# A decoder block on one core: two entries held back at the stage boundaries, and eight turns of the identity at the start

## The chip, the cores and the metric

The kernel runs on one core of a Trainium2 chip. A core has engines with a queue of instructions each, which run beside one another and wait for each other through semaphores: TensorE (PE in the profile, its weight loads PEld), VectorE (DVE), ScalarE (ACT), GpSimd (POOL) and SyncE (SP, which here only issues DMAs). An engine takes its own instructions in order, so one that waits holds up all behind it. The metric is the device time of one execution in microseconds.

## The reference

One layer of a hybrid decoder on x of 256 tokens by 2048 channels, all in float32:

```python
x = layer_norm(ALPHA * x + 0.5 * swiglu(x, ffn1...), ln1_g, ln1_b)
mix = concat(attention(x @ w_in), rg_lru(x @ w_in)) @ w_out
x = layer_norm(ALPHA * x + mix, ln2_g, ln2_b)
x = layer_norm(ALPHA * x + 0.5 * swiglu(x, ffn2...), ln3_g, ln3_b)
x = x + sigmoid(x @ w_ple_gate) * (p @ w_ple_proj)
```

swiglu is (silu(x @ gate) * (x @ up)) @ down with a width of 5632. The layer norm is taken over the 2048 channels of a token: mean and variance, then a scale and a shift per channel. Each stage needs the normalised output of the stage before.

## The kernel before, in words

**Numbers in two halves.** TensorE multiplies in a rounded float32 format. Each operand is therefore split into hi (its rounded value, a cast on ScalarE, line 104) and lo (the rest, a subtraction on VectorE, line 109), and a product is hi*hi + hi*lo + lo*hi.

**The plan.** All weights stand in one list, self.plan, in the order in which they are used. An entry is 256 rows by 512 columns, 512 KB. load() issues its DMA into a raw tile (10 of them), prepare_hi() casts, prepare_lo() subtracts. Most entries put hi and lo into two pools of 7 slots (SLOTS); entries marked "work" put them into the pool of 11 work tiles (w4, "w" in the rows) that the stages use for their intermediate results too. Work entries are the third and fourth of the last eight of a down projection, and the first three of the next stage.

**Who prepares when.** take() hands out the next entry and calls advance(), done() gives its slot back and calls it too. advance() goes up to AHEAD = 7 entries beyond those taken, bounded by self.limit and by free slots, and issues the lo split one entry behind the hi cast:

```python
end = min(self.limit, self.taken + AHEAD)
while self.ready < end and (self.plan[self.ready]["work"] or self.live < SLOTS):
    self.prepare_hi(self.ready)
    self.ready += 1
    self.advance_lo(self.ready - 1 if self.taken else self.ready)
```

prepare_hi(q) also issues the loads of all entries below q + 5. The order of the instructions on each engine is the order in which the Python code issues them (manual_schedule); a tile from a pool waits for the last use of the tile that had its place.

**A stage boundary, down_last (line 492).** The last 512 rows of a down projection (ffn1, w_out, ffn2: three calls) are eight entries: for each of four blocks n of 512 columns, two. The first loop takes them and sums token tile 0 (128 tokens): down_mm(acts, es[n], 0, n, False) is 12 matmuls into one bank, into_acc (line 385) adds the bank to acc on VectorE, ln_stats (513) takes statistics. ln_norm (515) aggregates them, GpSimd raises to the power -0.5 (522), and VectorE normalises acc in four pieces (525). The second loop does token tile 1 with the same entries; halfway through its block 1 TensorE transposes the first four blocks of normalised tile 0 (ln_transpose, 535: four transposes into a bank, ScalarE scales and shifts, line 538, then casts and VectorE subtracts into xT, lines 64 and 65), and after blocks 1, 2 and 3 the rest. Entries are given back in the second loop, so done() prepares more there.

**After a boundary.** The next stage begins with eight entries on token tile 0 alone (group_b with boundary=True), and transposes tile 1 during the last four of them (HOOKS); after the second call of swiglu, ple_proj with four entries comes first, which needs p and not xT. split_p, which splits p into one work tile, is part of preparing its first entry.

**The start.** setup() (line 640) writes the identity with GpSimd; self.ident is used for all transposes. Then the first entries and xT are loaded, cast and split, and TensorE begins with group_a.

Of the kernel before, what the change touches and what calls it, by code (L numbers as in the profile page):

```python
# [12 lines left out]
P = 128  # L13
# [27 lines left out]
class Block:  # L41
# [449 lines left out]

    def down_last(self, acts):
        es, st = [], [self.tile(self.small, [P, 4, 6], F32, "bst") for _ in range(2)]
        for n in range(4):
            es.append([self.take(), self.take()])
            self.down_mm(acts, es[n], 0, n, False)
            self.ln_stats(st[0], 0, n)
        self.ln_norm(st[0], 0)
        for n in range(4):
            self.down_mm(acts, es[n], 1, n, False, mid=(lambda: self.ln_transpose(0, 0)) if n == 1 else None)  # L500
            self.ln_stats(st[1], 1, n)
            if n < 3:
                for e in es[n]:
                    self.done(e)
            if n > 0:
                self.ln_transpose(0, n)
        self.ln_norm(st[1], 1)
        for e in es[3]:
            self.done(e)
# [130 lines left out]
    def setup(self):  # L640
        nc, i = self.nc, self.i
        c = self.const
        self.ident = c.tile([P, P], F32, name="ident")
        make_identity(nc, self.ident)
        self.mhalf = c.tile([P, 1], F32, name="mhalf")
        nc.gpsimd.memset(self.mhalf, -0.5)
        self.par = c.tile([P, 192], F32, name="par")
        self.trig = c.tile([P, 2, 2, 16], F32, name="trig")
        self.dec = c.tile([P, 2, 12], F32, name="dec")
# [359 lines left out]
```

## Time and profile before

| | us |
|---|---|
| median of 3 timed runs | 1912.32 (1910.5 to 1912.78) |
| the profiled execution | 1905.79 |
| its span, first to last instruction | 1904.0 |
| TensorE busy (share of the span) | 1868.5 (98%) |
| VectorE busy | 1494.9 (79%) |
| ScalarE busy | 1077.8 (57%) |
| mean granted TensorE clock | 0.995 |

The profile is of one execution. "Busy" is the time in which an engine had an instruction under way; matmuls are pipelined and their ends are modelled, so consecutive ones overlap in the rows (389 ns printed, 0.23 from start to start for 512 columns). What an engine waits for is read from the views of waits and from the instructions in order of time, where idle time before an instruction and what ended it stand in brackets. The releaser named is the one that came last by the profile, which can be a neighbour of the true one.

### The profile page before, as it was taken

How to read it: one execution, taken by the hardware profiler on the slowest of the kernel's cores; microseconds unless marked ns; L12 is line 12 of the kernel's file. 1: busy time of each engine (PE TensorE's matmuls, PEld its weight loads, DVE VectorE, ACT ScalarE, POOL GpSimd, SP SyncE). 2: the span in 40 equal slices, each digit the busy share in tenths (PEclk: the TensorE clock that was granted, in tenths of full speed). 3: DMA queues.
4: the chain of work that ended last, by engine and by line, in shares of the span. 5: the costliest groups of instructions: out<-in, count | busy, mean ns of one | idle time of the engine just before them, and what ended most of it. 6: DMA issues, size and time to landing. Idle time of an engine off the chain costs nothing.

```text
span 1904.0 us, 26424 instructions
## 1 busy us (share of the span) xinstructions
PE 1868.5 (98%) x9844; PEld 1603.2 (84%) x9844; DVE 1494.9 (79%) x1910; ACT 1077.8 (57%) x1422; POOL 124.2 (7%) x108
## 2 busy tenths in 40 slices
PE   8999999999999989999999899999999999999899
PEld 7888888888888878887888788888888888888687
DVE  6698887887888876688677867878879888788674
ACT  6565555555655646555755455655556556556552
POOL 0001010100010000011100000101000101010000
PEclk9999999999999999999999999999999999999999
DMA  9678687788786857565455575887887878778381
GB/s 354 232 198 264 203 257 235 207 260 247 211 255 209 266 178 231 175 185 158 138 184 187 167 243 155 250 231 211 258 247 207 255 211 253 243 198 276 131 263 44
DMA packets 214593, 413.02 MB, mean 217 GB/s; under 512 B 13104, under 2 KB 15808, under 8 KB 214464
## 3 DMA queue, kind: packets, MB, share of 16 engines
q1 hardware_dynamic: 193856, 370.42, 58.1%
q0 software_dynamic: 20608, 40.91, 12.6%
q8 instruction: 77, 1.26, 0.3%
q14 instruction: 52, 0.43, 0.1%
HBM read 409.18 MB, written 2.10 MB: 216 GB/s over the span
## 4 chain that ended last, share of the span: by engine, by line
PE 95%; DVE 2%; ACT 1%; issue 1%; DMA 0%; SPq 0%; POOL 0%; DVEq 0%; POOLq 0%; ACTq 0%
PE mm L264 94%; DVE lo L109 1%; PE mm L535 1%; DMA raw<-in_ffn_w_gate_dram 0%; ACT hi L104 0%; DVE w L109 0%; DVE bst L513 0%; DVE acc L385 0%; PE mm L792 0%; DVE raw L82 0%; DVE w L721 0%; DVE w L65 0%; ACT w L64 0%; POOL rs L522 0%; DVE w L627 0%
## 5 line engine op out<-in xcount | busy, mean ns | idle before, releaser
L104 ACT CAST hi<-raw 128x1024 fp32r<-128x1024 f32 (+1 forms) x774 | 797.2, 1049 | 556.4 <-PE mm L264 501.2
L264 PE MATMUL mm<-xT,hi 128*128 128x512 f32 x3072 | 1057.6, 391 | 5.6 <-ACT hi L104 5.6
L109 DVE TENSOR_TENSOR lo<-raw,hi 128x1024 fp32r<-128x1024 f32 (+1 forms) x774 | 915.2, 1221 | 93.4 <-ACT hi L104 84.5
L264 PE MATMUL mm<-xT,lo 128*128 128x256 f32 x3072 | 850.5, 277 | 0.1
L264 PEld LDWEIGHTS mm<-xT,hi 128*128 128x128 f32 x3072 | 577.5, 188 | 127.2 <-ACT hi L104 5.8
L264 PEld LDWEIGHTS mm<-xT,lo 128*128 128x128 f32 x3072 | 577.7, 188 | 6.3 <-DVE lo L109 1.3
L264 PE MATMUL mm<-hi,w 128*128 128x512 f32 x1480 | 481.6, 391 | 1.8 <-DVE acc L435 1.2
L264 PEld LDWEIGHTS mm<-hi,w 128*128 128x128 f32 x1480 | 277.9, 188 | 63.7 <-ACT hi L104 1.5
L264 PE MATMUL mm<-lo,w 128*128 128x512 f32 x740 | 289.5, 391 | 0.0
L264 PE MATMUL mm<-hi,xT 128*128 128x512 f32 (+1 forms) x648 | 200.9, 385 | 0.0
L264 PEld LDWEIGHTS mm<-lo,w 128*128 128x128 f32 x740 | 139.1, 188 | 23.9
L85 POOL DMA_DIRECT2D raw<-in_ffn_w_down_dram x72 | 86.6, 1214 | 1080.7 <-DVE raw L82 547.7
L437 DVE TENSOR_TENSOR acc<-acc,mm 128x512 f32<-128x512 f32 x110 | 75.2, 684 | 98.6 <-PE mm L264 98.6
L264 PEld LDWEIGHTS mm<-hi,xT 128*128 128x128 f32 x648 | 120.3, 188 | 23.1
L264 PE MATMUL mm<-lo,xT 128*128 128x512 f32 (+1 forms) x324 | 123.6, 382 | 0.0
L378 DVE TENSOR_TENSOR w<-mm,w 128x256 f32<-128x256 f32 x192 | 80.2, 419 | 20.5 <-ACT w L377 20.0
L82 DVE TENSOR_TENSOR raw<-raw,raw 128x1024 f32<-128x1024 f32 x72 | 87.9, 1221 | 1.2
L377 ACT COPY w<-mm 128x256 f32<-128x256 f32 x192 | 69.6, 364 | 21.2 <-PE mm L264 17.2
L64 ACT CAST w<-qk 128x512 fp32r<-128x512 f32 (+1 forms) x42 | 25.5, 609 | 86.4 <-DVE qk L482 46.0
L612 ACT ACTIVATE w<-w 128x256 f32<-128x256 f32 x84 | 35.1, 418 | 66.3 <-DVE w L378 66.3
L264 PEld LDWEIGHTS mm<-lo,xT 128*128 128x128 f32 x324 | 61.0, 188 | 11.2
L613 DVE TENSOR_TENSOR w<-w,w 128x256 f32<-128x256 f32 x84 | 35.8, 426 | 41.4 <-ACT w L612 41.4
(139 smaller groups left out, 788.0 us busy)
## 6 DMA issues: line engine op xcount, KB each, us to landing
raw<-in_ffn_w_up_dram SPq DMA_DIRECT2D x176, 512.0 KB, 4.9
raw<-in_ffn_w_down_dram SPq DMA_DIRECT2D x176, 512.0 KB, 5.3
raw<-in_ffn_w_gate_dram SPq DMA_DIRECT2D x175, 512.0 KB, 6.0
raw<-in_w_in_dram SPq DMA_DIRECT2D x88, 512.0 KB, 4.6
raw<-in_ffn_w_down_dram POOLq DMA_DIRECT2D x72, 512.0 KB, 7.6
raw<-in_w_out_dram SPq DMA_DIRECT2D x32, 512.0 KB, 4.4
raw<-in_w_ple_gate_dram SPq DMA_DIRECT2D x32, 512.0 KB, 5.6
w<-in_ln_g_dram SPq DMA_DIRECT2D x12, 256.0 KB, 7.4
```

What stands on the lines that cost most here:

```text
L64: self.nc.scalar.copy(hi, src)
L82: self.nc.vector.tensor_tensor(a, a, b, op=ALU.add)
L85: self.nc.gpsimd.dma_start(a, src, accum_op=ALU.add)
L104: self.nc.scalar.copy(e["hi"][:, k, :], e["raw"][:, k, :])
L109: self.nc.vector.tensor_tensor(e["lo"][:, k, :], e["raw"][:, k, :], e["hi"][:, k, :].bitcast(F32), op=ALU.subtract)
L264: self.nc.tensor.matmul(out, lhsT=lhsT, rhs=rhs, start=start, stop=stop, skip_group_check=True)
L377: self.nc.scalar.copy(c, bank[:, 256:])
L378: self.nc.vector.tensor_tensor(dst, bank[:, :256], c, op=ALU.add)
L437: self.nc.vector.tensor_tensor(a, a, bank, op=op)
L535: nc.tensor.transpose(bank[:, q * P:(q + 1) * P], self.acc[:, t, kb * P:(kb + 1) * P], self.ident)
L612: nc.scalar.activation(s, g, AF.Sigmoid)
L613: nc.vector.tensor_tensor(g, g, s, op=ALU.mult)
```

## The change

In down_last self.limit is set to ten entries beyond those taken, eight of its own and two of the next stage, before the first loop, and lifted after ln_norm of token tile 0. In setup a PSUM bank is taken and TensorE transposes the identity into it eight times; nothing reads that bank.

```diff
     def down_last(self, acts):
         es, st = [], [self.tile(self.small, [P, 4, 6], F32, "bst") for _ in range(2)]
+        self.limit = self.taken + 10
         for n in range(4):
             es.append([self.take(), self.take()])
             self.down_mm(acts, es[n], 0, n, False)
             self.ln_stats(st[0], 0, n)
         self.ln_norm(st[0], 0)
+        self.limit = len(self.plan)
         for n in range(4):
             self.down_mm(acts, es[n], 1, n, False, mid=(lambda: self.ln_transpose(0, 0)) if n == 1 else None)
             self.ln_stats(st[1], 1, n)
@@
         make_identity(nc, self.ident)
+        bank = self.bank()
+        for _ in range(8):
+            nc.tensor.transpose(bank[:, :P], self.ident, self.ident)
         self.mhalf = c.tile([P, 1], F32, name="mhalf")
```

## Rows read from the trace of the kernel before

**Rows 1.** The chain of work that ended last: share of the span by engine.
```profile
PE 95%; DVE 2%; ACT 1%; issue 1%; DMA 0%; SPq 0%; POOL 0%; DVEq 0%; POOLq 0%; ACTq 0%
```
**Rows 2.** TensorE's waits: waiter, releaser, us in total, times, longest.
```profile
PE mm L535 <- DVE acc L525: 19.1, 3, 8.0
```
**Rows 3.** TensorE in order of time, first call: start, us, instruction [idle before <-releaser].
```profile
696.56 0.62 PE L264 MATMUL mm<-hi,w 128*128 128x512 f32 x2
...
699.51 1.52 PE L264 MATMUL mm<-w,w 128*128 128x512 f32 x6
706.62 1.11 PE L535 MATMUL mm<-ident,acc 128*128 128x128 f32 x4 [5.59 <-DVE acc L525]
...
723.67 0.60 PE L535 MATMUL mm<-ident,acc 128*128 128x128 f32 x4
```
**Rows 4.** VectorE in order of time, first call.
```profile
700.90 1.23 DVE L109 TENSOR_TENSOR w<-raw,w 128x1024 fp32r<-128x1024 f32 x1 [6.92 <-PE mm L264]
...
703.37 0.67 DVE L385 TENSOR_TENSOR acc<-acc,mm 128x512 f32<-128x512 f32 x1
...
706.01 1.92 DVE L525 TENSOR_SCALAR acc<-acc,mv,rs 128x512 f32<-128x512 f32 x4 [0.76 <-POOL rs L522]
707.84 0.68 DVE L385 TENSOR_TENSOR acc<-acc,mm 128x512 f32<-128x512 f32 x1
...
709.17 2.34 DVE L109 TENSOR_TENSOR lo<-raw,hi 128x1024 fp32r<-128x1024 f32 x2
...
719.22 0.69 DVE L65 TENSOR_TENSOR xT<-qk,xT 128x512 fp32r<-128x512 f32 x1 [0.81 <-ACT xT L64]
...
720.94 1.92 DVE L525 TENSOR_SCALAR acc<-acc,mv,rs 128x512 f32<-128x512 f32 x4 [0.67 <-POOL rs L522]
```
**Rows 5.** VectorE in order of time, third call.
```profile
1780.64 1.23 DVE L109 TENSOR_TENSOR w<-raw,w 128x1024 fp32r<-128x1024 f32 x1 [8.71 <-ACT hi L104]
```
**Rows 6.** TensorE in order of time, second and third call.
```profile
1077.26 1.11 PE L535 MATMUL mm<-ident,acc 128*128 128x128 f32 x4 [5.49 <-DVE acc L525]
...
1788.80 1.11 PE L535 MATMUL mm<-ident,acc 128*128 128x128 f32 x4 [8.03 <-DVE acc L525]
```
**Rows 7.** A stretch: us, PE busy (instructions), granted clock, DMA share, GB/s.
```profile
706.60:710.00 3.40, 3.38 (x11) 0.52 0.00 0
```
**Rows 8.** The chain in order of time, three calls: start, us, what.
```profile
707.73 2.42 PE mm L264 x6
710.15 0.44 PE mm L535 x4
...
726.09 1.40 PE mm L264 x6
...
1078.38 2.56 PE mm L264 x6
1080.94 0.85 PE mm L535 x4
...
1789.91 2.35 PE mm L264 x6
```
**Rows 9.** All engines in order of time, the start.
```profile
1.02 0.29 POOL masks.py:199 TENSOR_SCALAR_AFFINE_SELECT ident<-ident 128x128 f32<-128x128 f32 x1
...
5.17 0.77 PE L264 MATMUL mm<-xT,hi 128*128 128x512 f32 x1 [5.17 <-ACT hi L104]
...
9.19 1.04 ACT L104 CAST hi<-raw 128x1024 fp32r<-128x1024 f32 x1 [1.05 <-DMA raw<-in_ffn_w_gate_dram]
9.23 0.63 PE L264 MATMUL mm<-xT,hi 128*128 128x512 f32 x1
...
9.87 0.51 PE L264 MATMUL mm<-xT,hi 128*128 128x512 f32 x1
...
10.27 1.22 DVE L109 TENSOR_TENSOR lo<-raw,hi 128x1024 fp32r<-128x1024 f32 x1 [1.41 <-ACT hi L104]
...
11.54 0.38 PE L264 MATMUL mm<-xT,lo 128*128 128x256 f32 x1
```

## The prediction

> **What bounds the kernel now.** I read the chain of waits first: TensorE holds 95% of it [rows 1]. So only two things can move the time: a wait of TensorE, or a stretch in which it runs slowly. The list of TensorE's waits has one large entry: three waits of L535 (the transposes of a normalised token tile) for L525 (the normalisation on VectorE), 19.1 us together, the longest 8.0 [rows 2]. They are the first transposes in the three calls of down_last. I call the calls A (about 690 to 735 us), B (1062 to 1100) and C (1769 to 1825), number the ten or so plan entries from a call's start 0, 1, 2, ... (0 to 7 are its own, 8 on belong to the next stage), and write (t, n) for the twelve matmuls of token tile t and column block n.
>
> In A TensorE ends (0,3) with the matmul started at 696.56, goes on with (1,0) and the first half of (1,1), and should transpose at 699.51 + 6 x 0.23 = 700.9; it does so at 706.62, after 5.59 idle [rows 3]. The VectorE rows say why [rows 4]: the lo split of entry 10 ("w<-raw,w") sits idle 6.92 us until 700.90, waiting for TensorE, and behind it in the queue stand into_acc and bn_stats of (0,2) and (0,3), the aggregate and the normalisation (706.01). (0,2) was finished on TensorE by 694.3 (696.56 less twelve matmuls at 0.23, and its own end). The releaser's time is the end of the first half of (1,1), the last reader of entry 2, which lies in the same pool of work tiles as entry 10: the split waits for that tile. So VectorE does no normalising until TensorE has used up everything that does not need it.
>
> **Part 1, the limit.** take() prepares up to seven entries ahead, so before the change entries 8 to 11 are prepared while tile 0 is summed. With the limit at ten, entries 10 and 11 go behind ln_norm. One more thing goes with them: the lo split is issued one entry behind the hi cast, so lo 9 is only issued when entry 10 is prepared. Ahead of ln_norm VectorE therefore keeps lo 8 and loses lo 9 and lo 10. This matters in C, where it is lo 9 that blocks (8.71 idle, start 1780.64 [rows 5]); there split_p takes one more work tile.
>
> New order on VectorE in A: lo 8, into_acc and bn_stats of (0,1), (0,2), (0,3) as TensorE delivers them. (0,3) can be added at about 697.0 (last matmul 696.56 + 0.43). From that instruction to the normalisation took 706.01 - 703.37 = 2.64, so it starts at 699.6, its first quarter (1.92/4, printed 0.56 in the chain) is out at 700.2, and TensorE arrives at 700.9 [rows 3, 4]. The 5.59 goes, with 0.6 to spare. B and C run the same matmuls in the same order, so 5.49 and 8.03 go as well [rows 6]. Sum of the waits: **19.1**.
>
> The waits cost more than their idle time. After the one in A the granted clock is 0.52 from 706.60 to 710.00, the lower of the two levels (1.2 against 2.4 GHz); the engine had stood still for 5.59 us before [rows 7]. In the chain the four transposes take 1.11 instead of 0.44, and the six matmuls after them 2.42 in A, 2.56 in B, 2.35 in C instead of 1.40; B's next four transposes take 0.85 [rows 8]. That is (0.67 + 1.02) + (0.67 + 1.16 + 0.41) + (0.67 + 0.95) = **5.6**, and without an idle stretch it goes.
>
> What the moved work costs. It is not removed: after into_acc and bn_stats of (1,0), the two done() calls now issue lo 9, 10, 11, 12 where lo 11 and 12 stood. hi 10 to hi 13 keep their order on ScalarE (no other ScalarE instruction lies between), and the loads theirs on SP's queue; raw 9 and raw 10 are held longer, but the loads that reuse them are for entries 19 and 20. lo 9 and lo 10 may now wait for entry 2's tiles, free at 700.9, while VectorE reaches them at 702.8. Two more splits are 2.3 us by the pair at 709.17 [rows 4]. into_acc of (1,0) moves from 707.84 to 701.5, 6.4 earlier; all that follows on VectorE moves 6.4 - 2.3 = 4.1 earlier, and the 0.81 idle at 719.22 closes, so the second normalisation starts at 720.94 - 4.9 = 716.0 and its first quarter is out at 716.6. TensorE gains 5.6 + 1.7 = 7.3 and reaches the first transposes of tile 1 at 723.67 - 7.3 = 716.4 [rows 3, 4]. So VectorE is next late, by some 0.2 to 0.3. B has the same order of work on both engines and is charged alike: **0.7** for the two, with the restart. In C ple_proj lies between (it needs no tile of xT): nothing. Worked on with the same durations, the split of xT's first block of tile 0 ends at about 708 (needed by the next stage at 709.7), entries 14 and 15 are split by 719.1 and 720.2 (needed at 718.7 and 720.5): covered, or short by tenths. If the cover is less, each us of VectorE's lateness costs A and B one us.
>
> **Part 2, the eight turns.** They start when the identity is there (1.02 + 0.29 = 1.31 [rows 9]). Four transposes at the low clock took 1.11 [rows 3], so eight end near 3.6, before the first matmul, which waits for data until 5.17 [rows 9]; even at 0.47 each unoverlapped they end at 5.1. Cost 0. Gain: an early pair of matmuls (512 and 256 columns) takes 0.64, as 9.23 to 9.87 shows, about twice what the six of rows 8 suggest at the higher clock, and between 7.6 and 9.87 there are three and a half pairs: about 1.0 us of TensorE time. But the next entry's weights land at 9.17, ScalarE casts from 9.19, VectorE splits from 10.27 to 11.50, and TensorE's idle ends at 11.54 with exactly that split [rows 9]; a faster TensorE waits longer for it. So 0, with bounds 0 and 1.0 gained (if that load lands an us earlier in another run).
>
> The Trainium skill speaks against this part: "TensorE: Matmul & The Clock Gate", Part 4 on the PE-mode transpose, says that transposes do not count as TensorE activity for the clock. By it the first real matmuls still take 0.64 a pair and the gain is 0 in every run; if it does not hold here, up to the 1.0 above is there for the taking. No row of before has transposes alone, so the trace does not decide; the forecast is 0 either way.
>
> **Sum.** 19.1 + 5.6 - 0.7 + 0 = 24.0 us. The profiled execution took 1905.8 (1904.0 span): 1881.8 there. The timed runs have a median of 1912.3, 6.5 above it, and I see no row that says what the 6.5 is; taking 24.0 from the median gives **1888.3**. Bounds: the waits alone with no clock gain and two us of lateness in A and B, 19.1 - 4 = 15; everything, with the start's 1.0 and no lateness, 25.7.
>
> **Rivals.**
> 1. VectorE's tail is later than I make it (a hi cast of 10 or 11 that must wait for entry 2's tiles puts four casts of 1.05 ahead of tile 0's evacuation, 0.9 later at the second normalisation in each of A and B; or lost tenths elsewhere). For it: slack of a few tenths only. Two of the three calls lose 0.9 to 1.9 each: 20 to 22 us gained, 21 in the middle: 1891.3. Chance 0.17.
> 2. The limit does not free the blocked split everywhere: if lo 9 stayed ahead of the sums, C would keep its wait but for one split (1.2 gained instead of 9.6), 15.6 in all: 1896.7. Against: the one-entry lag of the lo splits is in the code and in the order of rows 4 (lo 10 after hi 11). Chance 0.06.
> 3. It gets slower: a moved split gets a work tile that is free only at the end of (1,3), 709.1 in the new time, and holds VectorE with tile 0's xT behind it. Then xT of block 0 is ready at 713.1 instead of 707.9 and TensorE waits 3.6, then about 2 more at tile 1's transposes, and 1.7 for the clock; with the release 1 us later still A loses more than its 7.3. For all three calls: 1914 to 1917. It decides from a release at 709 on. For it: the pool is at its limit in the trace (6.92 and 8.71 idle). Against: entry 2's two tiles are free at 700.9 and entry 3's at 702.7, and only lo 9, hi 10 and lo 10 need any. Chance 0.03.
> 4. No difference: the waits go, and as much comes back at tile 1's transposes. That would need six more us on VectorE there than I count: 1912. Chance 0.02.
>
> **How the numbers follow.** Forecast 0.72, rivals 0.17, 0.06, 0.03, 0.02. About 0.2% (3.8 us) is what a measurement of this kernel can tell from no change. Faster 0.95 (forecast, rivals 1 and 2), same 0.02, slower 0.03. The range: the forecast's own, 24.0 -1.7 +1.7 +- the runs' spread (1905.8 to 1912.8 shows that a median may lie 6 lower), is 1882 to 1892; reaching to rivals 1 and 2 makes it 1882 to 1897.
>
> **What would show it.** Right: no wait of L535 for L525 above 1 us; the clock at 1.00 through all three calls; VectorE's split before the sums only lo 8; four lo splits after into_acc of (1,0); the first transposes of a call directly after the sixth matmul of (1,1). For part 2: matmuls of the first entry at 0.34 or 0.64 a pair, and TensorE's steady run starting at 11.5 in both cases. Wrong: a wait of more than 1 us at tile 1's transposes or at the next stage's first matmuls, or a start earlier than 11.

## The result, and the profile after

| | before | after |
|---|---|---|
| median of 4 timed runs | 1911.41 us (1909.25 to 1912.78) | 1885.42 us (1883.78 to 1885.59) |
| the profiled execution | 1905.79 us | 1883.78 us |
| its span | 1904.0 us | 1882.0 us |

The ratio is 0.9863, 95% interval 0.9846 to 0.988: 26.0 us less in the medians, 22.9 to 29.4 by the interval (0.012 and 0.0154 of 1911.4). Between the two profiled executions it is 22.0 us. The forecast was 1888.3 us, that is 24.0 less than the 1912.3 of three runs; the time lies in the range of 1882 to 1897.

The page of the changed kernel: granted clock in 40 slices, shares of the chain that ended last.

```profile
PEclk9999999999999999999999999999999999999999
...
PE 95%; DVE 2%; ACT 1%; DMA 1%; issue 1%; SPq 0%; ACTq 0%; DVEq 0%
```

The shares of the chain say nothing about the change: TensorE holds 95% before [rows 1] and after. The list of TensorE's waits, read next, does: here are its longest entries in the changed kernel (waiter, releaser, us in total, times, longest). The transposes of L535 stand at L537 now, the normalisation of L525 at L527.

```profile
PE mm L264 <- DVE xT L65: 1.7, 1, 1.7
PE mm L264 <- ACT w L798: 1.6, 1, 1.6
```

No entry of L537 is left in it, where 19.1 us stood [rows 2]. The windows around the calls A, B and C of the changed kernel (us, TensorE busy and instructions, granted clock, DMA share, GB/s) show that the slow stretches behind the waits [rows 7] went too:

```profile
684.00:735.00 51.00, 51.00 (x241) 1.00 0.50 160
1060.00:1105.00 45.00, 45.00 (x215) 1.00 0.51 156
1765.00:1825.00 60.00, 60.00 (x282) 1.00 0.62 206
```

How it went is seen in call A. VectorE of the changed kernel, in order of time (start, us, instruction, idle before and its releaser):

```profile
691.32 1.21 DVE L109 TENSOR_TENSOR w<-raw,w 128x1024 fp32r<-128x1024 f32 x1
...
698.00 0.69 DVE L385 TENSOR_TENSOR acc<-acc,mm 128x512 f32<-128x512 f32 x1 [1.30 <-PE mm L264]
...
700.67 1.91 DVE L527 TENSOR_SCALAR acc<-acc,mv,rs 128x512 f32<-128x512 f32 x4 [0.76 <-POOL rs L524]
...
703.82 2.34 DVE L109 TENSOR_TENSOR w<-raw,w 128x1024 fp32r<-128x1024 f32 x2
706.08 2.35 DVE L109 TENSOR_TENSOR lo<-raw,hi 128x1024 fp32r<-128x1024 f32 x2
...
716.95 1.92 DVE L527 TENSOR_SCALAR acc<-acc,mv,rs 128x512 f32<-128x512 f32 x4 [0.67 <-POOL rs L524]
```

The split at 691.32 is lo 8. The next ones, lo 9 to lo 12 (two pairs, 703.82 and 706.08), stand behind the normalisation. The sums now wait for TensorE (1.30 before the last of them), not TensorE for the sums. Before, a split sat idle 6.92 us in this place and the normalisation began at 706.01 [rows 4].

TensorE of the changed kernel in the same call:

```profile
700.52 1.53 PE L264 MATMUL mm<-w,w 128*128 128x512 f32 x6
701.89 0.60 PE L537 MATMUL mm<-ident,acc 128*128 128x128 f32 x4
...
717.55 0.66 PE L537 MATMUL mm<-ident,acc 128*128 128x128 f32 x4
```

The transposes follow the first half of (1,1) with no idle time; before, 5.59 lay between and the four took 1.11 [rows 3]. The first transposes of tile 1 (717.55) are the next thing that VectorE holds up, by tenths: the first quarter of the normalisation that starts at 716.95 is out just before them, and in the chain the four take 0.64 instead of 0.44. The chain of the changed kernel, with the six matmuls after the transposes at 1.39 in all three calls, where it had 2.42, 2.56 and 2.35 [rows 8]:

```profile
702.05 0.44 PE mm L537 x4
702.49 1.39 PE mm L264 x6
...
717.57 0.64 PE mm L537 x4
...
1066.22 1.39 PE mm L264 x6
...
1081.30 0.55 PE mm L537 x4
...
1768.87 1.39 PE mm L264 x6
```

The start of the changed kernel, TensorE and ScalarE:

```profile
1.37 1.97 PE L649 MATMUL mm<-ident 128*128 128x128 f32 x8 [1.37 <-POOL mhalf L651]
...
5.08 0.77 PE L264 MATMUL mm<-xT,hi 128*128 128x512 f32 x1 [1.75 <-DVE xT L65]
...
12.54 0.62 PE L264 MATMUL mm<-xT,hi 128*128 128x512 f32 x1
...
13.12 0.40 PE L264 MATMUL mm<-xT,hi 128*128 128x512 f32 x1
...
51.57 0.37 ACT L377 COPY w<-mm 128x256 f32<-128x256 f32 x1
```

The eight turns take 1.97 us and end before the first data come. Matmul pairs start 0.64 apart up to 12.54 and 0.34 to 0.35 apart from 13.12 on. By the start of the first pair that is less than 0.5 from the next, the quick pairs begin at 13.1 here and at 9.9 in the profile of before [rows 9], and the copy that stands here at 51.57 begins at 50.55 there.

**Where the 22.0 us of the two profiles came from.** I put the same instructions of both traces side by side; what the distance between them changes by in a stretch is what that stretch gained or lost.

| stretch | gained, us | forecast |
|---|---|---|
| start, up to the first half of (1,1) in A | -1.02 | 0 |
| call A | 7.02 | 6.93 |
| call B | 7.70 | 7.38 |
| 1138 to 1186 us (1124 to 1174 in the changed kernel), matmul pairs 0.350 apart instead of 0.340 | -1.37 | none |
| call C | 9.66 | 9.65 |
| sum | 21.99 | 23.96 |

Forecast for A: 5.59 + 0.67 + 1.02 - 0.35; for B: 5.49 + 2.24 - 0.35; for C: 8.03 + 1.62.

### The profile page after: what moved, and what is told of

Its sections match the earlier page's. It is cut to its first block, busy times and chain, and to the rows that moved or that the text cites. A ratio compares the mean times of both kernels' runs of the same rounds, so it can differ in the third digit from the quotient of the medians.

```text
span 1882.0 us, 26440 instructions
## 1 busy us (share of the span) xinstructions
PE 1867.3 (99%) x9852; PEld 1602.3 (85%) x9852; DVE 1494.4 (79%) x1910; ACT 1077.4 (57%) x1422; POOL 124.2 (7%) x108
## 4 chain that ended last, share of the span: by engine, by line
PE 95%; DVE 2%; ACT 1%; DMA 1%; issue 1%; SPq 0%; ACTq 0%; DVEq 0%
PE mm L264 94%; DVE lo L109 1%; PE mm L537 1%; ACT hi L104 1%; DMA raw<-in_ffn_w_down_dram 0%; DMA raw<-in_ffn_w_gate_dram 0%; PE mm L797 0%; DVE w L378 0%; DVE raw L82 0%; DVE w L726 0%; DVE w L65 0%; ACT w L64 0%; DVE w L629 0%; ACT w L614 0%; ACT L748 0%
```

## The experiments

The theory: the limit alone makes the gain, because VectorE's queue no longer has a split in it that waits for a work tile of entry 2; of the gain 19.1 is idle time of TensorE and 5.6 is its clock after the idle time; the turns do nothing. The rivals: the turns have a part in it (a gain or the 1.0 us lost at the start), the clock term is something else, the limit works because VectorE has less work and not because a blocked split went. S1 and S2 in the expectations are two readings of the start's 1.0 us: S1, that the turns put off the rise of the clock; S2, that the start differs from run to run whatever the kernel.

### 1. The limit alone (e1_limit_only) and the turns alone (e2_turns_only)

```
     def down_last(self, acts):
...
+        self.limit = self.taken + 10
...
         self.ln_norm(st[0], 0)
+        self.limit = len(self.plan)
```

```
         make_identity(nc, self.ident)
+        bank = self.bank()
+        for _ in range(8):
+            nc.tensor.transpose(bank[:, :P], self.ident, self.ident)
```

> The limit without the eight turns. If the limit does it all, the three calls gain 7.0, 7.7 and 9.7 us as in the changed kernel and the ratio to the kernel before is 0.986 to 0.988. Theory S1 (the turns hold the clock's rise back): the early matmul pairs go from 0.64 to 0.34 near 9.9 us as in the kernel before, the first group's reads of its bank end near 50.5, and the run is 1.0 us faster than the changed kernel. Rival S2 (the rise falls at another time from run to run, turns or not): the rise lies anywhere between 9 and 13 us and the start is 0 to 1.0 us late here too. Rival of the whole: if the turns carried part of the gain, it is under 20 us.

> The eight turns without the limit. Theory: no gain. The three waits stay at 5.6, 5.5 and 8.0 us, ratio 0.999 to 1.001. S1: the clock rises near 12.9 us again and the run is 1.0 us longer than the kernel before. S2: the rise lies anywhere from 9 to 13. If the turns did warm the clock, the pairs would take 0.34 from the first one at 5 us on.

Measured: the limit alone 1884.68 us (1883.39 to 1886.01), ratio 0.9865 (0.9852 to 0.9878); the turns alone 1910.04, ratio 1.0002 (0.9993 to 1.0011), beside 1909.87 for the kernel before. TensorE's waits with the turns alone:

```profile
PE mm L535 <- DVE acc L525: 19.1, 3, 8.0
```

It is the entry of before, unchanged. And TensorE at the start with the limit alone, without turns:

```profile
12.50 0.63 PE L264 MATMUL mm<-xT,hi 128*128 128x512 f32 x1
...
13.57 0.40 PE L264 MATMUL mm<-xT,hi 128*128 128x512 f32 x1
```

Without any turn the pairs get quick at 13.1, as late as in the changed kernel's profile, so the late start does not need the turns and S1 has no support. The gain is the limit's; the turns are worth nothing, within 0.1%.

### 2. The wait filled with matmuls (e5_fill)

The kernel before, with matmuls into a bank that nothing reads put in front of the first transposes of each call, as many as fill the wait. They change no output.

```
+        def mid():
+            bank = self.bank()
+            for _ in range(35 if self.which == 2 else 24):
+                self.mm(bank, acts[0][:, 2, P:], es[1][1]["hi"][:, 0, :], True, True)
+            self.ln_transpose(0, 0)
...
-            self.down_mm(acts, es[n], 1, n, False, mid=(lambda: self.ln_transpose(0, 0)) if n == 1 else None)
+            self.down_mm(acts, es[n], 1, n, False, mid=mid if n == 1 else None)
```

> The kernel before, with extra matmuls (24, 24 and 35, into a bank that nobody reads) in TensorE's wait before the first transposes of each call: the waits stay, but TensorE is not idle in them. If the 5.6 us that I put on the clock is right, the granted clock stays at 1.00 through the three calls, the first four transposes take 0.44 us instead of 1.11 and the next six matmuls 1.40 instead of 2.42, 2.56 and 2.35, and the run is 5 us shorter (ratio 0.997 to 0.998). Rival: the slow transposes and matmuls after the wait come from something else (VectorE's and ScalarE's reads beside them); then they stay slow and the ratio is 1.000 or more.

Measured: 1904.26 us (1902.13 to 1905.79) beside 1909.87; ratio 0.9969 (0.9957 to 0.9981), 5.6 us less. Two windows of this kernel, the first that of [rows 7], and its chain in A:

```profile
706.60:710.00 3.40, 3.26 (x20) 1.00 0.02 5
...
1778.00:1790.00 12.00, 11.91 (x57) 1.00 0.26 89
```

```profile
706.75 0.66 PE mm L541 x4
707.40 1.39 PE mm L264 x6
```

The transposes come at 706.75, as late as before (706.62), but the engine was kept at work until then. The granted clock stays 1.00 where it was 0.52, and the six matmuls take 1.39 instead of 2.42; the four transposes take 0.66, better than 1.11 but not the 0.44 expected. So the second term of the sum is what it was called: time that TensorE loses in the slower of its two levels because it stood still before. Without touching the wait 5.6 us can be had, 3.6 to 8.2 by the interval; in the two profiles the three calls are 5.1 shorter.

### 3. The limit one higher and one lower (e3_limit_11, with the turns; e4_limit_9, without)

```
+        self.limit = self.taken + 11
```

```
+        self.limit = self.taken + 9
```

> One size changed: the limit at eleven entries instead of ten, with the turns. Only entry 11 is held back, but lo 10 with it, since the lo split goes one entry behind; lo 9 stays ahead of the sums. Theory: the first two calls gain as in the changed kernel (lo 9 is not blocked there), the third keeps its wait, since there lo 9 is the blocked split: 7 of 8 us of idle remain and the clock falls. Gain 15 to 16 us, ratio 0.992. Rival (any two entries fewer is enough, or one): ratio 0.986 to 0.988. Rival (lo 10 is blocked by something other than its tile): no gain in the first two.

> One size changed the other way, without the turns: the limit at nine, so entry 9 goes behind the normalisation too, and lo 8 with it; five splits instead of four follow the sum of (1,0). Theory (VectorE is next late, an us of lateness costs an us in the first two calls): second normalisation 1.1 us later, the wait at tile 1's first transposes grows from 0.3 to about 1.5 us in the first two calls, nothing in the third: 2.3 us longer than the limit at ten, ratio 0.988 to 0.989. Rival (VectorE has slack there): same time as with ten.

Measured, with 11: 1893.67 us beside 1910.04, ratio 0.9912 (0.9897 to 0.9927). With lo 9 ahead of the sums again, A and B have no wait of the transposes left and C keeps its own. VectorE, then TensorE, in C of this kernel:

```profile
1770.06 1.22 DVE L109 TENSOR_TENSOR w<-raw,w 128x1024 fp32r<-128x1024 f32 x1 [8.71 <-ACT hi L104]
```

```profile
1777.08 1.11 PE L537 MATMUL mm<-ident,acc 128*128 128x128 f32 x4 [6.89 <-DVE acc L527]
```

The idle time of lo 9 is to the hundredth that of before (8.71 [rows 5]); the transposes wait 6.89 instead of 8.03 because lo 10 is no longer behind it. The row names a cast as what ended the idle time, but that is a neighbour: the casts of entries 8 to 10 had run by 1757.1, and lo 9 starts 1.39 after the first half of (1,1) begins (1768.67), as the blocked split of before does in A (699.51 and 700.90 [rows 3, 4]). The gain is 16.4 us; the prediction's second rival, worked out for just this case, had 15.6.

Measured, with 9: 1886.32 us, ratio 0.9875 (0.986 to 0.9889), 1.6 more than the limit of ten alone (1884.68, on another chip). The intervals of the two ratios overlap, so the profile has to decide. One more entry is put off, and its split comes in front of the second normalisation in A and B. TensorE's waits in this kernel, and the first transposes of tile 1 in A:

```profile
PE mm L537 <- DVE acc L527: 2.2, 2, 1.1
```

```profile
718.12 0.66 PE L537 MATMUL mm<-ident,acc 128*128 128x128 f32 x4 [1.15 <-DVE acc L527]
```

The work of one split (1.2 us) that VectorE gets between the two normalisations turns into 1.15 and 1.04 us of TensorE's waiting; A and B together gain 2.3 less than in the changed kernel's profile, as expected. So at ten VectorE is just in time there: this is the price of lateness that the prediction named, and it had the right place.

### 4. One work tile more, and no limit (e8_one_more_tile, with its control e9_raw_9)

The kernel before with twelve work tiles instead of eleven; room was made by nine raw tiles instead of ten, and the control has the nine raw tiles alone.

```
-RAWS = 10
+RAWS = 9
...
-            tc.tile_pool(name="work", bufs=11) as self.work,
+            tc.tile_pool(name="work", bufs=12) as self.work,
```

> The kernel before, without limit and turns, with one work tile more (12) and, to make room, one raw tile less (9). Theory (what blocks VectorE is that the lo half of a held-ahead entry has no work tile until TensorE has read entry 2): in the first two calls lo 10 gets the added tile, is split while tile 0 is summed, and the waits of 5.6 and 5.5 us and the low clock after them go, 15 us together; in the third call, which needs one tile more, lo 9 gets it and lo 10 is blocked in its place, so most of the 8 us stays. Gain 16 us or a little more, ratio 0.991 to 0.992, unless nine raw tiles cost something (the kernel beside this one shows that). Rival (the splits ahead of the sums are simply too much work for VectorE before the normalisation): the waits stay in all three, ratio 1.000.

> The control for the run beside it: the kernel before with nine raw tiles and the work tiles as they were. Expected: the three waits as before (5.6, 5.5, 8.0 us); the loads start up to one entry later, hidden by the seven entries ahead: ratio 1.000, or up to 1.003 if TensorE then waits for loads.

Measured: the control 1909.48 us, ratio 0.9994 (0.9985 to 1.0004), with the waits of before. The twelfth tile: 1893.1 us beside 1911.22, ratio 0.9907 (0.989 to 0.9923). Its VectorE in A, and in C:

```profile
693.43 1.21 DVE L109 TENSOR_TENSOR w<-raw,w 128x1024 fp32r<-128x1024 f32 x1
```

```profile
1766.44 1.23 DVE L109 TENSOR_TENSOR w<-raw,w 128x1024 fp32r<-128x1024 f32 x1 [6.25 <-PE mm L264]
```

No VectorE instruction was moved or taken away, and the split of entry 10 runs in A with no idle time at all, ahead of the normalisation as before. In C the call takes one tile more than the others, and there entry 10 takes entry 9's place as the one that waits (6.25; TensorE's wait for the normalisation is 5.6). This is the direct evidence that the split was blocked by the pool of work tiles: with a tile to take, the work ahead of the sums costs A and B nothing.

### 5. lo 9 put back into VectorE's idle time (e7_lo9_early)

The limit without the turns, and in A and B lo 9 issued between the statistics of (0,1) and the sums of (0,2), where VectorE now waits for TensorE.

```
         for n in range(4):
             es.append([self.take(), self.take()])
+            if n == 2 and self.which < 2:
+                self.advance_lo(self.ready)
```

> The limit without the turns, and in the first two calls lo 9 issued between the statistics of (0,1) and the sum of (0,2), where VectorE of the changed kernel stands idle 1.3 us. Theory (VectorE's tail is what is late at tile 1's transposes, by one split more than it need be): the second normalisation comes 1.1 us earlier, the 0.3 to 0.4 us of lateness at tile 1's first transposes goes in both calls, and the run is 0.5 us shorter than the limit alone, too little for the timing to tell. Rival (lo 9 is blocked there as well): VectorE idles before it and the waits of 5 us come back in both calls, 10 us or more.

Measured: 1884.37 us (1882.58 to 1884.55) beside 1884.68 for the limit alone on the same chip; ratio to before 0.9861 (0.9848 to 0.9875). VectorE at the new place of lo 9, then TensorE at tile 1's first transposes, in A of this kernel:

```profile
694.77 1.21 DVE L109 TENSOR_TENSOR w<-raw,w 128x1024 fp32r<-128x1024 f32 x1
```

```profile
718.27 0.60 PE L539 MATMUL mm<-ident,acc 128*128 128x128 f32 x4
```

lo 9 fills an idle stretch, and the transposes take 0.60 where the changed kernel's took 0.66. The mechanism is as expected, but what it is worth (tenths in each of two calls) is below what the runs can tell. It is as quick as the changed kernel, not shown to be quicker.

### 6. Real matmuls in place of the turns (e6_matmul_warm)

With the limit, and the identity multiplied by itself eight times in f32 (sixteen records) instead of turned.

```
+        bank = self.bank()
+        for _ in range(8):
+            self.mm(bank[:, :P], self.ident, self.ident, True, True)
```

> The changed kernel with eight plain float32 matmuls of the identity in place of the eight turns. If TensorE's clock rises for matmuls and not for transposes, the granted rate is up earlier: pairs at 0.34 from about 6 to 8 us on, the first group's bank read out near 50.5, because the weights' splits still end TensorE's idle time at 11.5; 1.0 us shorter than the changed kernel. Rival S2 (the rise falls where it falls): pairs slow until 9 to 13 us. No forecast of a gain over the limit alone: the first loads bound the start.

Measured: 1884.51 us, ratio 0.9863 (0.9847 to 0.988), the same as the changed kernel. TensorE at the start of this kernel, and the granted clock of a window there:

```profile
1.36 3.79 PE L264 MATMUL mm<-ident 128*128 128x128 f32 x16 [1.36 <-POOL mhalf L651]
...
8.00 0.49 PE L264 MATMUL mm<-xT,hi 128*128 128x512 f32 x1 [1.80 <-ACT hi L104]
...
9.29 0.39 PE L264 MATMUL mm<-xT,hi 128*128 128x512 f32 x1
...
10.20 0.63 PE L264 MATMUL mm<-xT,hi 128*128 128x512 f32 x1
```

```profile
9.50:13.00 3.50, 3.50 (x13) 0.53 1.07 383
```

Matmuls do what the turns do not: the pairs that start at 8.95 and 9.29 are 0.34 apart, where those of the changed kernel are still 0.64 apart at 12. But the engine stood waiting for data before 8.00, and at about 9.7 the clock falls again (0.53) and rises at 13.1. Nothing is won in the time; that the data come too late to keep the engine at work is argued from these rows, no run tests it. The Trainium skill ("TensorE: Matmul & The Clock Gate", Part 4 on the PE-mode transpose) says that full speed does not engage for a transpose, which does not count as busy in the same way, and these rows agree: eight of them, 1.97 us of busy time, brought quick pairs in no profile before 10.6, sixteen matmul records of 3.79 us brought them by 8.95. The two differ in length and in the idle time behind them (1.75 and none) as well as in kind, so the kind alone is not shown by this pair.

### 7. The changed kernel once more (e10_changed_again)

> The changed kernel once more, for a second profile of its start. S1 (the turns hold the clock's rise back): a rise near 12.9 us again. S2 (it falls where it falls): anywhere from 9.9 to 13.3 us, as the kernels so far with and without turns have it. In both: ratio 0.986, the three calls without a wait over 0.5 us. The pairs of matmuls between 1124 and 1174 us, 0.350 us each in the first profile where the kernel before has 0.340: if that is a state of the run, they may be at 0.340 here; if it belongs to the program, 0.350 again.

Measured: 1882.81 us (1881.17 to 1884.34), ratio 0.9852 (0.9837 to 0.9867). In this profile, of the very same kernel, the quick pairs begin at 10.6 instead of 13.1 and the copy of 51.57 starts at 50.45. Over all profiles but that of experiment 6 they begin, without turns, at 9.6, 9.9, 9.9, 10.3, 10.8, 11.8 and 13.1, with turns at 10.6, 11.1, 13.0 and 13.1. S2 stands: the start's 1.02 us in the table above belongs to that one execution. Seven starts against four do not exclude that the turns put the rise off a little.

## Why the prediction was right

**The waits, 19.1 us.** Right, and for the reason given. The blocked split was read from the rows as one waiting for entry 2's tile; experiment 4 frees it by a tile and experiment 3 puts only C's back. The new time of the normalisation in A was worked out as 699.6; it is 700.67, and all of the 1.0 is that TensorE itself comes 1.02 later from the start. The slack of 0.6 that the working gave it was enough in all three calls.

**The clock, 5.6 us.** Right in cause: experiment 2 wins it with the wait left in place. The size is that of one execution, and that experiment 2 gives 5.6 to the tenth is luck, with an interval of 3.6 to 8.2. The kernel with the turns alone has the same three waits, but in its profile the work behind them is slow for longer. The chain in A after the first transposes: of before, what follows on the lines of [rows 8]; then the same stretch with the turns alone. There the six matmuls take 2.56 instead of 2.42, the next transposes 0.85 instead of 0.44 and the twelve matmuls behind them 3.27 instead of 2.76:

```profile
710.58 2.76 PE mm L264 x12
```

```profile
709.94 2.56 PE mm L264 x6
712.50 0.85 PE mm L535 x4
713.35 3.27 PE mm L264 x12
```

Counted like the prediction's term, with the twelve matmuls that follow, the slow work costs 5.7 us in the profile of before, 7.4 in that of the nine raw tiles and 8.7 in this one, for the same 19.1 us of waits.

**VectorE's lateness at tile 1, -0.7 us.** The place is right, the size too large. The second normalisation was put at 716.0, 717.0 with the start's shift, and starts at 716.95. The four transposes take 0.64 in A and 0.55 in B instead of 0.44. In the table A lacks 0.26 of its waits and clock (7.28 - 7.02) and B 0.03 (7.73 - 7.70): 0.3 together. Experiment 3 at nine shows that there was no more to spare, as reckoned.

**C with nothing to pay.** 9.66 measured, 9.65 reckoned.

**The turns, 0.** Right: experiment 1. The reason given did not come: the split at 11.5 was to hold TensorE up whatever its clock, and in neither profile of the changed kernel does TensorE stand idle there. What the profile alone seemed to say, 1.02 lost at the start, would have been a wrong lesson from one execution.

**The rivals.** Rival 1 did not come: the casts of entries 10 and 11 did not wait (that of 11 begins at 688.20 in A without idle time), and the tail is 0.3 where it needed 0.9 to 1.9 a call. Rival 2 is a true mechanism, which a limit of eleven brings about (16.4 against its 15.6), not one of ten. Rival 3 needed the moved split to wait for a tile until the end of (1,3); lo 9 and lo 10 run at 703.82 without idle time. Rival 4 needed six us of lateness where 0.3 was found.

**What the sum did not hold.** The three calls give 24.4 in the profiles (24.0 forecast), the timed medians 26.0. The 1.6 between lie within the interval of the measurement. The prediction said that it saw no reason for the 6.5 us between the profiled execution of before and its median. The runs show two parts of one. That execution is the quickest of all that were taken of the kernel before, and its matmul pairs are at the quicker of two rates in both stretches that can have either (last section). And it has less time at the lower clock than most: of the 36 timed executions of the kernel before in the experiments, the eight with a mean granted clock of 0.995, which the profile has too, have a median of 1908.51 us, the nineteen with 0.993 one of 1911.86; the changed kernel has 0.999 or 1.000 in every one. So the forecast took a clock term read from a cheap execution off a median that holds dearer ones. That fits a gain above 24.0, but how the 1.6 divide is not shown.

## What to carry to other kernels

When a wait stands on an engine's list, look at what is queued ahead of the releasing instruction on its own engine: here the normalisation was not slow, it stood behind a split that waited for a buffer which only the waiting engine could free, and putting that split behind the urgent work, or giving it one more buffer, ended the wait alike (the buffer in two of the three calls; in the third the next split waited in its place). Price such a wait with the slow stretch after it (5.6 to 8.7 us on 19.1 here, by execution), and price the moved work at the next place where that engine is nearly late. Before blaming a part of a change for a microsecond at the start of one profile, look at a second profile of the same kernel.

## What the runs showed of the hardware beyond that

Matmuls of the same shapes ran at two rates with the same granted clock of 1.00. Pairs of 512 and 256 columns, before and after:

```profile
1137.58 0.39 PE L264 MATMUL mm<-xT,hi 128*128 128x512 f32 x1
1137.80 0.28 PE L264 MATMUL mm<-xT,lo 128*128 128x256 f32 x1
1137.92 0.39 PE L264 MATMUL mm<-xT,hi 128*128 128x512 f32 x1
```

```profile
1124.20 0.39 PE L264 MATMUL mm<-xT,hi 128*128 128x512 f32 x1
1124.43 0.28 PE L264 MATMUL mm<-xT,lo 128*128 128x256 f32 x1
1124.55 0.40 PE L264 MATMUL mm<-xT,hi 128*128 128x512 f32 x1
```

From start to start it is 0.34 in the first and 0.35 in the second; over the stretch the means are 0.340 and 0.350. The same shows in the number of instructions of a window, first of before, then of the limit alone:

```profile
60.00:90.00 30.00, 30.00 (x179) 1.00 0.58 189
```

```profile
60.00:90.00 30.00, 30.00 (x173) 1.00 0.62 203
```

In the profiles a rate holds for a whole stretch: from the clock's rise at the start to about 107 us (0.350 or a little more with the limit alone, the turns alone, the limit of eleven, the real matmuls, lo 9 early and the nine raw tiles; 0.340 in the other six) and from 1124 to 1174 us of the changed kernel, the same matmuls in the others (0.340 in before, in the nine raw tiles and in the changed kernel's second profile; 0.350 in the rest). Both kinds occur with and without either part of the change, and in two profiles of one kernel (the changed one, in the second stretch). The first stretch is worth up to some 2.3 us, the second 1.4. What sets the rate is open; no run was made for it.
